# Moving conditioning rows between the first three feed-forwards, and their loads to another queue

## The chip, the cores and the metric

The kernel runs on one core of one Trainium2 chip. The metric is the device time of one execution in microseconds (us). A core has five engines that run side by side: TensorE (PE in the profile) multiplies matrices, VectorE (DVE) and ScalarE (ACT) work elementwise, GpSimd (POOL) does so more slowly, and SyncE (SP) only issues DMA transfers. Each engine takes its own instructions in a fixed order and waits at the first one that isn't ready. Transfers are carried out by 16 DMA engines, whichever engine issued them.

## The reference, cut to what matters

Two layers with their own weights are applied to 128 context tokens and 512 latent tokens of width 1024. Each layer is feed-forward, token mixing, feed-forward, and each of these three has its own shift, scale and gate, which come from the conditioning vector:

```python
def layer(x, cond, p, ...):
    mods = (silu(cond) @ p['w_ada'] + p['b_ada']).reshape(cond.shape[0], 9, 1, D_MODEL)
    sh1, sc1, g1, sh2, sc2, g2, sh3, sc3, g3 = [mods[:, i] for i in range(9)]
    h = modulate(rmsnorm(x, p['norm_ffn1']), sh1, sc1)
    x = x + 0.5 * g1 * swiglu(h, p['w_ffn1_in'], p['w_ffn1_out'])
    h = modulate(rmsnorm(x, p['norm_mix']), sh2, sc2)
    y, kv = token_mix(h, p, ...)
    x = x + g2 * y
    h = modulate(rmsnorm(x, p['norm_ffn2']), sh3, sc3)
    x = x + 0.5 * g3 * swiglu(h, p['w_ffn2_in'], p['w_ffn2_out'])
```

`swiglu` has a hidden width of 2816. The product of the conditioning with `w_ada` gives 9216 values per layer and conditioning vector; there are two vectors, one for context and one for latent tokens.

## The kernel before, in words

**Stages.** The kernel runs, in time, feed-forward 1 (layer 0, about 20 to 531 us in the profile), mixing 1, feed-forward 2 (layer 0, about 821 to 1303 us), feed-forward 3 (layer 1, about 1303 to 1745 us), mixing 2, and feed-forward 4 (layer 1, about 2033 to 2475 us). All 640 tokens lie on the free axis, and the whole activation stays on the chip; the weights stream past in loads of 128x512 floats (`load_raw`, line 159, issued by SP, nine buffers).

**A feed-forward** (`ffn`) treats the 22 column blocks of the hidden width one after the other; one such block is a *pair* here (gate and up part). The pairs are cut into five parts of 5, 5, 4, 4 and 4 (`PARTS`). After each part come eight *outputs* (line 517 and 528), which multiply the part's activations with the output weights and add the result to `x`. So a feed-forward is ten stretches in turn: pairs 1, outputs 1, ..., pairs 5, outputs 5. The residual update of the outputs needs the gate, so the gate must be known before outputs 1. The last outputs also prepare the next norm (`nx.tile`).

Every float32 weight and activation is split in two numbers of fewer bits, `hi` on ACT and `lo` on DVE (lines 174 and 175), and three products are made. DVE also forms sums of weight blocks (line 608), takes results out of the accumulators and applies the gating (lines 622 to 642 and 550).

**Conditioning rows.** The products with `w_ada` that aren't needed at the very start are made on DVE, in *steps* (`ada_steps`, lines 268 and 270). A step loads 128x1024 floats of `w_ada` (512 KB) into one of two buffers (tag `KS`, which the mixing uses too), and multiplies and sums them with each of the two conditioning vectors: two long DVE instructions. Four steps make a chunk of 512 of the 9216 columns; chunks 2j and 2j+1 hold row j of the nine. Steps wait in a list (`Pump`), and `ffn` takes them from it: a pair counts 2 and an output 1, times the feed-forward's rate in `RATES`, and whenever the sum reaches 1 a step is written into the program. A feed-forward counts 22 x 2 + 40 = 84 in all. The loads were issued by SP, in one queue with the weights.

**Order on an engine.** The framework's planner fixes each engine's order when the program is built: whenever an engine comes free by its estimate, it takes the instruction that is ready and stands earliest in the program's text. So a step can run earlier than its place in the text, in a gap that the planner sees on DVE. At run time the order is fixed.

Of the kernel before, what the change touches and what calls it, by code (L numbers as in the profile page):

```python
# [22 lines left out]
POOLD = ()  # L23
SHO = range(8)
SPREAD = 3
RATES = (0.8, 0.8, 0.55)
WLATE = 4
P1A, P0B, P1B = 1, 2, 2
D = 1024
# [53 lines left out]
def hybrid_step(ctx: ExitStack, tc: tile.TileContext, x_in, cc_in, cb_in, w_ada0, w_ada, pv_in, lam_in, w_fin, w_fout, w_min, w_mout,  # L83
                cache_in, ident_in, rope_in, cnt_in, sel_in,
                y_out, ngk, ngv, ndk, ndv):
    nc = tc.nc
    V, S, G, PE = nc.vector, nc.scalar, nc.gpsimd, nc.tensor
# [13 lines left out]
    def nm(s):  # L101
        uid[0] += 1
        return f"{s}_{uid[0]}"
# [4 lines left out]
    def T(dt=F32):  # L108
        return tp.tile([128, UW], dt, tag="t", name=nm("t"))
# [11 lines left out]
    def PS():  # L121
        return psS.tile([128, 2, 512], F32, tag="S", name=nm("S"))

    def PH():
        return psH.tile([128, 512], F32, tag="H", name=nm("H"))

    def PF():
        return psF.tile([128, 512], F32, tag="F", name=nm("F"))

    def C(shape, dt=F32, name="c"):  # L130
        n = nm(name)
        return const.tile(shape, dt, tag=n, name=n)
# [17 lines left out]
    def raw_tile():  # L150
        return wp.tile([128, 512], F32, tag="raw", name=nm("raw"), bufs=RAWB)

    def load_raw(src):

        n, r = src.shape[-1], []
        for c in range(0, n, 512):
            w = min(512, n - c)
            t = raw_tile()
            nc.sync.dma_start(t[:, :w], src[:, c:c + w])
            r.append(t[:, :w])  # L160
        return r

    class Weights:
# [5 lines left out]
        @staticmethod  # L169
        def piece(src, eng=None):  # L170
            n = src.shape[-1]
            hi = wp.tile([128, 512], F32R, tag="hi", name=nm("hi"), bufs=HLB)
            lo = wp.tile([128, 512], F32R, tag="lo", name=nm("lo"), bufs=HLB)
            S.activation(hi[:, :n], src, AF.Copy)  # L174
            (eng or V).tensor_tensor(out=lo[:, :n], in0=src, in1=hi[:, :n], op=ALU.subtract)  # L175
            return hi, lo
# [45 lines left out]
    mods = [[None] * 18 for _ in range(L)]  # L222

    def bada(l, c):
        b = PV_BADA + l * 72 + 4 * c
        return pv[:, b:b + 4].unsqueeze(2).to_broadcast([128, 4, 2])
# [33 lines left out]
    def ada_steps(l, c):  # L260
        m = []

        def step(b):
            if b == 0:
                m.append(C([128, 4, 2], name="mod"))
            t = sp.tile([128, 1536], F32, tag="KS", name=nm("wa"), bufs=2)
            raw, dump = t[:, :D], t[:, D:].bitcast(mybir.dt.bfloat16)
            nc.sync.dma_start(raw, w_ada[l, 4 * c + b])
            for i, o in enumerate((dump, raw)):
                V.scalar_tensor_tensor(out=o, in0=raw, scalar=1.0, in1=rows[i], op0=ALU.mult, op1=ALU.mult,  # L270
                                       accum_out=m[0][:, b, i:i + 1])
            if b == 3:
                V.tensor_tensor(out=m[0], in0=m[0], in1=bada(l, c), op=ALU.add)
                mods[l][c] = m[0]

        return [lambda b=b: step(b) for b in range(4)]
# [10 lines left out]
    def gate_tiles(l, sub):  # L287

        if sub == 1:
            return [mods[l][2 * (3 * sub + 2) + h] for h in range(2)]  # L290
        r = []
        for h in range(2):
            t = C([128, 4, 2], name="gate")
            V.tensor_scalar(out=t, in0=mods[l][2 * (3 * sub + 2) + h], scalar1=-0.5, scalar2=None, op0=ALU.mult)
            r.append(t)
        return r
# [199 lines left out]
    def product(ps, piece, act, start):  # L496

        hi, lo = piece
        for k in range(4):
            w0, w1 = hi[:, k * 128:(k + 1) * 128], lo[:, k * 128:(k + 1) * 128]  # L500
            ah, al = act[k][:, 0], act[k][:, 1]
            for p, (w_, a) in enumerate(((w0, ah), (w0, al), (w1, ah))):
                PE.matmul(ps, w_, a, start=start and k == 0 and p == 0, stop=k == 3 and p == 2, skip_group_check=True)  # L503
# [28 lines left out]
    def ffn(l, sub, norm, nxt, pump, prate):  # L532
# [11 lines left out]
        def activation(i, g, u, cb):  # L544

            lb = HW + HN
            for a, b, c in ((0, NC, cb), (NC, lb, lb)):
                S.activation(g[:, a:b], g[:, a:b], AF.Silu, bias=g[:, c:c + 1])  # L548
            for a, b, c in ((0, NC, cb), (NC, lb, lb)):
                V.scalar_tensor_tensor(out=u[:, a:b], in0=u[:, a:b], scalar=u[:, c:c + 1], in1=g[:, a:b],  # L550
                                       op0=ALU.add, op1=ALU.mult)
            hi, lo = U(), E(F32R)
            split(*[t[:, :N].rearrange("p (h n) -> p h n", h=2) for t in (hi, lo)], FastNorm.view(u)[:, :, :HN])
            acts[i] = (hi, lo)
            tick(2.0)
# [43 lines left out]
        def pair(i, first):  # L599


            a11, a12 = load_raw(wi[i, 0])
            a21, a22 = load_raw(wi[i, 1])
            s3 = raw_tile()
            piece = Weights.piece

            def add(o, a, b):
                V.tensor_tensor(out=o, in0=a, in1=b, op=ALU.add)  # L608

            A, B, D = PF()[:, :HW], PH()[:, :HW], PS()[:, 0, :HW]  # L610
            g, u = T(), T()
            w = piece(a11)
            product(A, w, norm.get("B11"), True)
            S.activation(g[:, :HW], A, AF.Copy)
            w = piece(a12)
            add(s3, a11, a21)
            add(a21, a21, a22)
            add(a11, a21, a11)
            product(B, w, norm.get("B21"), True)
            if first:  # L620
                norm.stats_sum()
            V.tensor_tensor(out=g[:, :HW], in0=B, in1=g[:, :HW], op=ALU.add)
            w = piece(a11)
            product(A, w, norm.get("N2"), False)
            S.activation(u[:, :HW], A, AF.Copy)
            w = piece(s3)
            add(a12, a11, a12)
            product(D, w, norm.get("T3"), True)
            S.activation(u[:, HW:], D, AF.Copy)
            if first:  # L630
                norm.stats_spread()
            w = piece(a21)
            product(A, w, norm.get("N1"), False)
            V.tensor_tensor(out=u[:, HW:], in0=A, in1=u[:, HW:], op=ALU.add)
            w = piece(a22)
            product(D, w, norm.get("T4"), False)
            V.tensor_tensor(out=u[:, :HW], in0=D, in1=u[:, :HW], op=ALU.add)
            w = piece(a12)
            product(A, w, norm.get("B22"), False)
            V.tensor_tensor(out=g[:, HW:], in0=A, in1=norm.R[:, HW:], op=ALU.mult)  # L640
            V.tensor_tensor(out=g[:, :HW], in0=g[:, :HW], in1=norm.R[:, :HW], op=ALU.mult)
            V.tensor_tensor(out=u, in0=u, in1=norm.R, op=ALU.mult)  # L642
            activation(i, g, u, HN)
# [64 lines left out]
        gate = None  # L708
        for k0, k1 in PARTS:
            for i in range(k0, k1):  # L710
                if l == 0 and sub == 0 and i < NPLAIN:
                    plain_pair(i)
                    if i == 0:
                        for k in range(4):
                            norm.late(k)
                else:
                    pair(i, i == 0)
            gate = gate or gate_tiles(l, sub)
            nx = nxt() if k1 == NP else None
            if k1 == NP and nx is None:  # L720
                last_out(k0, k1, gate)
            else:
                for d in ORDER:
                    out(k0, k1, d, gate, nx)
# [677 lines left out]
    nx = FastNorm(0, 0)  # L1402
# [24 lines left out]
    pump = Pump()  # L1427

    def ada_all(l, cs):
        for c in cs:  # L1430
            pump.add(ada_steps(l, c))

    ada_all(0, (4, 5, 8, 9, 6, 7, 10, 11, 14, 15, 12, 13))
    nx = ffn(0, 0, nx, lambda: Norm(0, 1), pump, RATES[0])
    pump.step(1000)
    cache = load_cache(0)
    lambdas()
    nx = mix(0, nx, lambda: FastNorm(0, 2), cache)
    cache = load_cache(1)
    rows = silu_rows()  # L1440
    ada_all(0, (16, 17))
    ada_all(1, (2, 3, 0, 1, 4, 5, 8, 9, 6, 7))
    nx = ffn(0, 2, nx, lambda: (pump.step(8), FastNorm(1, 0))[1], pump, RATES[1])
    pump.step(1000)
    ada_all(1, (10, 11, 14, 15, 12, 13, 16, 17))
    nx = ffn(1, 0, nx, lambda: Norm(1, 1), pump, RATES[2])
    pump.step(1000)
    nx = mix(1, nx, lambda: FastNorm(1, 2), cache)
# [113 lines left out]
```

## Time and profile before

| | |
|---|---|
| median of 3 runs | 2497.93 us (2492.87, 2497.93, 2497.96) |
| profiled execution | 2492.2 us, of which the span from first to last instruction is 2490.4 us |
| mean granted TensorE clock | 0.977 of full |
| busy share of the span: PE, DVE, ACT, POOL | 95%, 85%, 49%, 13% |

The terms of a forecast are read from the profiled execution. The three runs lie up to 5.1 us apart, so the comparison of two kernels goes by medians. An engine's busy share is a mean over stages with different limits.

### The profile page before, as it was taken

To read this page: it belongs to the slowest core of one execution; us is meant where nothing else is said; L and a number is where in the kernel's file an instruction comes from. 1 tells how busy PE (TensorE), PEld (TensorE's weight loads), DVE (VectorE), ACT (ScalarE), POOL (GpSimd) and SP (SyncE) were. 2 spreads that over 40 slices of the span, in tenths; PEclk is the share of its full clock that TensorE was granted. 3 is DMA by queue.
4 is the path that set the end of the run, shared out by engine and by line. 5 is a ranking of instruction groups with operands and counts; after the bars stand their busy time and mean duration, and the time that the engine had idled before them with its cause. 6 is when DMAs were issued, how large, how long until landed. Compare 5 with 4: busy or idle time off the path is not lost. (4 is left out here: it accounts for less than half of the span.)

```text
span 2490.4 us, 42262 instructions
## 1 busy us (share of the span) xinstructions
PE 2360.5 (95%) x15497; PEld 2290.3 (92%) x15497; DVE 2108.2 (85%) x3978; ACT 1213.3 (49%) x2447; POOL 315.2 (13%) x373
## 2 busy tenths in 40 slices
PE   7799999999998999998989999999999989999998
PEld 4798998999988899998979999999998979999997
DVE  5999998867887999999999998778588688767776
ACT  3534333457664634334355344445576565434434
POOL 3100000034233100000030000002422330000002
PEclk8999999999999999999989999999999989999999
DMA  7354443223423144554423453222243112223223
GB/s 267 109 169 139 156 156 117 86 80 122 136 75 123 60 153 125 160 161 147 128 81 104 155 150 96 69 85 85 76 154 105 51 39 80 82 78 97 81 73 98
DMA packets 142671, 280.70 MB, mean 113 GB/s; under 512 B 15360, under 2 KB 33664, under 8 KB 142464
## 3 DMA queue, kind: packets, MB, share of 16 engines
q1 hardware_dynamic: 142464, 278.01, 35.0%
q8 instruction: 122, 2.00, 0.3%
q14 instruction: 85, 0.70, 0.1%
HBM read 263.00 MB, written 14.94 MB: 112 GB/s over the span
## 5 line engine op out<-in xcount | busy, mean ns | idle before, releaser
L174 ACT ACTIVATE hi<-raw 128x512 fp32r<-128x512 f32 (+2 forms) x954 | 569.3, 605 | 874.2 <-PE S L135 359.4
L503 PE MATMUL F<-u,hi 128*128 128x322 f32 x2752 | 634.7, 318 | 33.0 <-ACT hi L174 31.1
L175 DVE TENSOR_TENSOR lo<-raw,hi 128x512 fp32r<-128x512 f32 (+1 forms) x874 | 565.2, 659 | 114.2 <-ACT hi L174 110.4
L135 PE MATMUL S<-u,hi 128*128 128x320 f32 (+3 forms) x2144 | 485.2, 317 | 35.5 <-DVE x L517 12.9
L503 PEld LDWEIGHTS F<-u,hi 128*128 128x128 f32 x2752 | 469.3, 192 | 41.7 <-ACT hi L174 34.3
L503 PE MATMUL F<-u,lo 128*128 128x322 f32 x1376 | 432.9, 315 | 10.5 <-DVE lo L175 10.5
L135 PE MATMUL S<-u,lo 128*128 128x320 f32 (+3 forms) x1776 | 419.3, 312 | 3.2 <-DVE lo L175 2.3
L135 PEld LDWEIGHTS S<-u,hi 128*128 128x128 f32 x2144 | 361.4, 193 | 46.9 <-issue 13.3
L270 DVE SCALAR_TENSOR_TENSOR wa<-wa,sc 128x1024 bf16<-128x1024 f32 (+1 forms) x264 | 323.5, 1233 | 9.7 <-DMA wa<-in_w_ada_dram 6.3
L135 PE MATMUL S<-e,hi 128*128 128x320 f32 (+2 forms) x1408 | 327.8, 310 | 1.1 <-DVE e L197 0.8
L503 PE MATMUL S<-u,hi 128*128 128x322 f32 x1376 | 316.1, 315 | 2.6 <-DVE x L528 2.3
L135 PEld LDWEIGHTS S<-u,lo 128*128 128x128 f32 x1776 | 305.1, 191 | 4.5 <-DVE lo L175 3.3
L503 PEld LDWEIGHTS F<-u,lo 128*128 128x128 f32 x1376 | 267.0, 194 | 13.8 <-DVE lo L175 13.1
L608 DVE TENSOR_TENSOR raw<-raw,raw 128x512 f32<-128x512 f32 x344 | 239.7, 697 | 5.2 <-DMA raw<-in_w_fin_dram 2.1
L135 PE MATMUL F<-u,hi 128*128 128x320 f32 (+1 forms) x1056 | 239.2, 318 | 1.5 <-DVE x L517 0.8
L503 PEld LDWEIGHTS S<-u,hi 128*128 128x128 f32 x1376 | 234.2, 191 | 5.7 <-ACT hi L174 5.0
L135 PEld LDWEIGHTS S<-e,hi 128*128 128x128 f32 x1408 | 236.6, 188 | 2.9 <-DVE e L197 2.5
L503 PE MATMUL S<-u,lo 128*128 128x322 f32 x688 | 215.3, 313 | 1.4 <-DVE lo L175 1.4
L528 DVE SCALAR_TENSOR_TENSOR x<-S,gate,x 128x128 f32<-128x128 f32 (+1 forms) x304 | 152.6, 544 | 53.0 <-PE S L135 52.1
L135 PEld LDWEIGHTS F<-u,hi 128*128 128x128 f32 x1056 | 178.6, 193 | 3.9 <-DVE x L517 0.8
L135 PE MATMUL F<-u,lo 128*128 128x320 f32 (+1 forms) x528 | 157.8, 318 | 0.0
L503 PE MATMUL H<-u,hi 128*128 128x322 f32 x688 | 156.0, 313 | 1.7 <-ACT hi L174 1.7
(229 smaller groups left out, 3032.8 us busy)
## 6 DMA issues: line engine op xcount, KB each, us to landing
raw<-in_w_fin_dram SPq DMA_DIRECT2D x352, 256.0 KB
wa<-in_w_ada_dram SPq DMA_DIRECT2D x132, 512.0 KB
raw<-in_w_fout_dram SPq DMA_DIRECT2D x168, 256.0 KB
raw<-in_w_min_dram SPq DMA_DIRECT2D x72, 256.0 KB
u<-in_w_ada_dram SPq DMA_DIRECT2D x24, 256.0 KB
KS<-kd SPq DMA_DIRECT2D x16, 384.0 KB
raw<-in_w_mout_dram SPq DMA_DIRECT2D x24, 256.0 KB
kd<-t SPq DMA_DIRECT2D x8, 640.0 KB
```

The source lines that it names most:

```text
L135: PE.matmul(out, lhsT, rhs, start=start, stop=stop)
L174: S.activation(hi[:, :n], src, AF.Copy)
L175: (eng or V).tensor_tensor(out=lo[:, :n], in0=src, in1=hi[:, :n], op=ALU.subtract)
L270: V.scalar_tensor_tensor(out=o, in0=raw, scalar=1.0, in1=rows[i], op0=ALU.mult, op1=ALU.mult, accum_out=m[0][:, b, i:i + 1])
L503: PE.matmul(ps, w_, a, start=start and k == 0 and p == 0, stop=k == 3 and p == 2, skip_group_check=True)
L528: V.scalar_tensor_tensor(out=x[d][:, a:b], in0=w[:, a:b], scalar=g[:, d % 4, c:c + 1], in1=x[d][:, a:b], op0=ALU.mult, op1=ALU.add)
L608: V.tensor_tensor(out=o, in0=a, in1=b, op=ALU.add)
```

## The change

The loads of the conditioning steps are issued by POOL (`G`) and no longer by SP. The rate of feed-forward 1 goes from 0.8 to 0.6 steps per count with the same 12 chunks, that of feed-forward 2 from 0.8 to 0.42 and from 12 chunks to 8, that of feed-forward 3 from 0.55 to 0.6 and from 8 chunks to 12. Since at the lower rates the chunks of the gate aren't complete when the gate is built, a loop takes steps from the list until they are. Before the norm that follows feed-forward 2, all that is left in the list is written out, and no longer 8 steps at most.

```diff
-RATES = (0.8, 0.8, 0.55)
+RATES = (0.6, 0.42, 0.6)
...
-            nc.sync.dma_start(raw, w_ada[l, 4 * c + b])
+            G.dma_start(raw, w_ada[l, 4 * c + b])
...
+            while gate is None and mods[l][2 * (3 * sub + 2) + 1] is None:
+                pump.step()
             gate = gate or gate_tiles(l, sub)
...
     ada_all(0, (16, 17))
-    ada_all(1, (2, 3, 0, 1, 4, 5, 8, 9, 6, 7))
-    nx = ffn(0, 2, nx, lambda: (pump.step(8), FastNorm(1, 0))[1], pump, RATES[1])
+    ada_all(1, (2, 3, 0, 1, 4, 5))
+    nx = ffn(0, 2, nx, lambda: (pump.step(1000), FastNorm(1, 0))[1], pump, RATES[1])
     pump.step(1000)
-    ada_all(1, (10, 11, 14, 15, 12, 13, 16, 17))
+    ada_all(1, (8, 9, 6, 7, 10, 11, 14, 15, 12, 13, 16, 17))
     nx = ffn(1, 0, nx, lambda: Norm(1, 1), pump, RATES[2])
```

## Rows read from the trace of the kernel before

**Rows 1.** The page's first part: busy time, share of the span, instructions.

```profile
PE 2360.5 (95%) x15497; PEld 2290.3 (92%) x15497; DVE 2108.2 (85%) x3978; ACT 1213.3 (49%) x2447; POOL 315.2 (13%) x373
```

**Rows 2.** Windows (length; PE, PEld, DVE, ACT, POOL busy; clock, DMA), feed-forwards 1 to 4.

```profile
167.80:444.90 277.10, 260.69 (x1718) 256.11 (x1717) 264.38 (x491) 108.01 (x203) 2.98 (x9) 0.99 0.43 135
926.80:1206.50 279.70, 263.12 (x1719) 258.29 (x1718) 274.14 (x506) 108.29 (x204) 1.84 (x6) 0.98 0.46 145
1403.60:1659.00 255.40, 255.38 (x1717) 254.14 (x1717) 218.50 (x398) 109.29 (x202) 2.10 (x7) 1.00 0.33 102
2139.70:2395.40 255.70, 255.37 (x1718) 253.50 (x1717) 194.01 (x343) 109.87 (x201) 0.00 (x0) 1.00 0.27 81
```

**Rows 3.** The same windows of feed-forwards 2 and 3, conditioning steps alone.

```profile
926.80:1206.50 279.70, 92.51 (x152) 0.98 0.46 145
1403.60:1659.00 255.40, 27.96 (x46) 1.00 0.33 102
```

**Rows 4.** Waits of PE, 920 to 1260 us: total, times, longest.

```profile
PE F L503 <- ACT hi L174: 10.9, 4, 3.5
PE F L503 <- DVE lo L175: 3.9, 3, 1.4
```

**Rows 5.** Windows, feed-forward 3, pairs 2 and outputs 2, columns as rows 2.

```profile
1403.60:1466.10 62.50, 62.50 (x421) 62.48 (x421) 61.83 (x113) 32.97 (x63) 1.92 (x4) 1.00 0.37 113
1466.10:1501.40 35.30, 35.30 (x243) 35.30 (x241) 34.39 (x69) 9.25 (x19) 0.18 (x3) 1.00 0.56 175
```

**Rows 6.** The two windows of rows 5, conditioning steps alone.

```profile
1403.60:1466.10 62.50, 11.03 (x18) 1.00 0.37 113
1466.10:1501.40 35.30, 16.93 (x28) 1.00 0.56 175
```

**Rows 7.** Windows, feed-forward 4 (no steps): pairs 2, pairs 4, outputs 4.

```profile
2139.70:2202.60 62.90, 62.90 (x423) 62.50 (x422) 53.96 (x95) 33.66 (x63) 0.00 (x0) 1.00 0.27 82
...
2316.60:2367.20 50.60, 50.47 (x339) 50.05 (x338) 41.40 (x72) 26.86 (x50) 0.00 (x0) 1.00 0.33 100
2367.20:2395.40 28.20, 28.17 (x193) 27.91 (x193) 18.45 (x33) 6.53 (x10) 0.00 (x0) 1.00 0.15 48
```

**Rows 8.** Windows, conditioning steps alone, mixing 1 to the end of feed-forward 2.

```profile
540.00:1178.00 638.00, 119.68 (x192) 0.98 0.38 124
1178.00:1305.00 127.00, 25.65 (x42) 0.96 0.34 109
```

**Rows 9.** Windows, feed-forward 1 from the third pair on; its outputs 5.

```profile
77.40:531.00 453.60, 424.17 (x2782) 416.80 (x2780) 422.71 (x782) 192.82 (x369) 23.34 (x38) 0.98 0.41 129
...
495.40:531.00 35.60, 35.33 (x237) 34.45 (x235) 29.27 (x47) 22.07 (x41) 17.10 (x25) 1.00 0.24 74
```

**Rows 10.** The conditioning buffers' instructions: ns min/median/max; idle before them (us, times).

```profile
L270 DVE SCALAR_TENSOR_TENSOR wa<-wa,sc x264: 1208/1217/2586, 38.5 to 1500.0; 128x1024 bf16<-128x1024 f32 x123, 128x1024 f32<-128x1024 f32 x9
...
  DMA wa<-in_w_ada_dram: 6.3, 6
```

**Rows 11.** Waits of SP's own queue, whole span: total, times, longest.

```profile
SPq L268 <- DVE wa L270: 453.9, 121, 19.3
```

**Rows 12.** Timeline of SP: issues in the start and in outputs 2 of feed-forward 3.

```profile
43.35 1.48 SPq L268 DMA_DIRECT2D wa<-in_w_ada_dram  x2
...
1491.76 0.33 SPq L268 DMA_DIRECT2D wa<-in_w_ada_dram  x1
```

**Rows 13.** Timeline of DVE: the first use of these two loads.

```profile
46.95 1.23 DVE L270 SCALAR_TENSOR_TENSOR wa<-wa,sc 128x1024 bf16<-128x1024 f32 x1 [2.48 <-DMA wa<-in_w_ada_dram]
...
1496.14 1.23 DVE L270 SCALAR_TENSOR_TENSOR wa<-wa,sc 128x1024 bf16<-128x1024 f32 x1 [0.40 <-DMA wa<-in_w_ada_dram]
```

**Rows 14.** POOL's smallest copies, whole span: ns min/median/max.

```profile
L423 POOL COPY t<-sh x32: 179/392/3382, 56.4 to 2034.4; 128x4 f32<-128x4 f32 x32
```

**Rows 15.** Windows, 5 us of the start, columns as rows 2.

```profile
20.00:25.00 5.00, 1.80 (x7) 1.12 (x7) 4.95 (x6) 5.00 (x13) 4.05 (x3) 0.95 1.04 396
```

**Rows 16.** Timeline of PE, where the first pair's second half begins.

```profile
52.65 0.91 PE L135 MATMUL S<-u,hi 128*128 128x322 f32 x2 [6.11 <-POOL u L416]
```

## Prediction

> **What bounds the kernel now.** The page's busy shares come first [rows 1]: PE is busy 95% of the span, so only what keeps PE waiting can move the end; DVE, at 85% on average, may do so in places. To see where, I cut the same work out of each feed-forward: pairs 2 to outputs 4, six stretches with equal matmuls [rows 2]. PE's count is 1717 to 1719 in all four, yet they take 277.1, 279.7, 255.4 and 255.7 us. The last two run at PE's own pace (PE busy 255.4 of 255.4 and of 255.7). The first two are longer by 21.6 and 24.2 us over a mean of 255.5, and there DVE is busy 264.4 of 277.1 and 274.1 of 279.7 us: in these stretches the end is set by DVE.
>
> What fills DVE is the conditioning steps: 92.5 us in that part of feed-forward 2, 28.0 us in feed-forward 3 [rows 3]. In the view of waits, PE waits for ACT's `hi` (10.9 us in four waits) and for DVE's `lo` (3.9 us in three) in feed-forward 2 [rows 4]; the same view of feed-forwards 3 and 4 lists no wait of PE in their stretch. 14.8 of the 24.2 us are these waits; I read the rest as short gaps and as matmuls after a wait at a lower clock (granted 0.98 against 1.00 [rows 2]).
>
> **Room on DVE.** A step is two instructions of about 1.22 us [rows 10], say 2.44 us. The windows by stretch show how many steps fit before PE has to wait. Pairs 2 of feed-forward 3: 61.83 us of DVE less 11.03 of steps leaves 50.8 of 62.5, room for 11.7 us, 4.8 steps; outputs 2: 34.39 less 16.93 in 35.3, 17.8 us or 7.3 steps [rows 5, 6]. PE was busy throughout in both, with 4.5 and 7 steps in them. From feed-forward 4: pairs of four blocks, 9.2 us or 3.8 steps; outputs after them, 9.75 us or 4.0 [rows 7]. Outputs 5, with the norm: 35.6 less 29.27, 2.6 steps [rows 9]. From outputs 1 to outputs 5 that is 7.3 + 4.8 + 7.3 + 3.8 + 4.0 + 3.8 + 4.0 + 3.8 + 2.6 = 41.4 steps.
>
> **The change part by part.**
>
> *Feed-forward 1, rate 0.8 to 0.6.* Its 48 steps stay. By the tenth count 8 were written before; now 6, and the new loop adds the other 2, since the gate (chunks 4 and 5) needs all 8. The remaining 40 were written by count 60, the end of pairs 4, which is 8 steps in pairs 2 (5 x 2 x 0.8) against room for 4.8; now they are spread to count 77, the start of outputs 5, with 6 in pairs 2. 40 fit into 41.4, so hardly anything is left over on DVE. The sum over the whole feed-forward says the same: 453.6 us with 422.7 of DVE [rows 9]; less 21.6 it would be 432.0, and DVE busy 97.8% of it, between the 98.9% and 97.4% that PE stood without a wait [rows 5]. That is the very edge, and steps that are written into a fixed place don't always meet a gap: I take 16 of 21.6 us, with ends 8 and 24 (above 21.6, since pairs 1 lose two steps, 4.9 us, to outputs 1).
>
> *Feed-forward 2, rate 0.8 to 0.42, 12 chunks to 8.* The 48 steps of before were done by 1178 us (192 instructions, four to a step, from 540 on), and then 42 more instructions, ten to eleven steps of feed-forward 3, ran before feed-forward 2 was over [rows 8]. So the planner draws steps forward into gaps, and what hurt is not how many there are but that those of feed-forward 2 stood ahead of the pairs' own work. With 32 steps at 0.42 that ends: after the gate's 8, 24 steps come to 3.4 in each outputs 1 and 2 and 4.2 in pairs 2, all below the room. Gaps are then filled from feed-forward 3. Of 24.2 us I take 23, ends 15 and 26.
>
> *Feed-forward 3, 8 chunks to 12.* 80 steps in both feed-forwards together stand against 8 for the gate plus twice about 41: they fit, as fill. Its pairs 3 to outputs 4, empty of steps now, get some 15. Filled stretches cost PE nothing in rows 5; I take +1, ends 0 and 6 (two steps too many, 4.9 us).
>
> *Loads from SP to POOL, 132 of them.* SP now stands 453.9 us in all, 121 times, before such a load until DVE frees one of the two buffers [rows 11], and the weight loads behind it stand too. That goes. It is worth little by itself, since feed-forward 3 has the same queue and no wait of PE; I count 0, ends 0 and -5, a part of the 10.9 us of `hi` waits [rows 4]. On POOL a load waiting for its buffer holds up what is behind it: nothing between the start and the last outputs (POOL busy 1.8 to 3.0 us in 277 [rows 2]), but there the squares and shift copies for the next norm (17.1 us of POOL in 35.6 [rows 9]), and in the mixings `lo` pieces. A planner that was right about DVE's times puts such a load where its buffer is free. Included in the next term.
>
> *How late a load lands.* From SP's issue to DVE's use, where DVE stood waiting: 3.6 us at the start and 4.4 us in outputs 2 [rows 12, 13]. DVE's waits for such loads are 6.3 us in the whole run [rows 10], so there is slack. No load is issued by POOL in this trace. The nearest row is POOL's smallest copy: 0.18 us at best, 0.39 in the median, 3.38 at worst [rows 14]; if POOL is held up like this when it issues, a load comes 0.2 to 3.2 us later. It matters in the outputs, where a step follows the other every 5 us: 7 + 7 + 4 + 4 + 2 in three feed-forwards, 72 steps. 0.2 us on each, none hidden, is 15 us. With the slack I take +2, ends 0 and 15. The Trainium skill, "SBUF — State Buffer", section "Who interferes with whom", speaks against this edit: a transfer issued from GpSimd has its descriptors written by GpSimd, which the port it shares with VectorE can starve, and it advises the other queues. It also says that VectorE's two-input operations, which fill DVE here, contend with GpSimd's reads and not its writes. The stretched copies of rows 14 agree with the first for reads; for loads no row here shows it. The same page's section "A bandwidth-pool intuition that's wrong" has a transfer of 0.62 us take 3.1 us beside a VectorE copy; 2.5 us on 72 steps would be an estimated 180 us.
>
> *Start.* In the first 35 us the DMA engines are full, near 400 GB/s [rows 15]. The first two conditioning loads no longer queue behind the activations and can go first: 1.05 MB, 2.6 us later for what PE waits for. The two after them lie in the chain that ends in a 6.11 us wait of PE [rows 16], DVE having waited 2.48 us for one [rows 13]; 3.2 us more at worst. I take +1, ends 0 and 6.
>
> **Sum.** -16 - 23 + 1 + 0 + 2 + 1 = -35 us on the span of 2490.4, so 2455.4, and 1.8 us more for the execution: 2457. The median of the runs is 5.7 us above the profiled execution; by it, 2497.9 - 35 = 2463. I forecast 2461.
>
> **The rivals.**
>
> *Feed-forward 1 gives nothing back.* For it: 40 steps in 41.4 is no room, and a burst of two stands ahead of its outputs 1. Against: nothing else of its cost grows. Without the 16 us: 2497.9 - 19 = 2479. With the ends of the small terms, 2485.
>
> *POOL's loads come late, slower.* Place: the outputs' 72 steps. DVE takes its instructions in order, so each microsecond that it stands for a load delays the residual updates and `lo` pieces behind it, and PE has two accumulators there. 35 / 72 = 0.5 us per step beyond the slack undoes the gain. If one load in four is held like the longest copy, 0.8 us on average, it is 58 us: 2497.9 - 37 + 58 = 2519. For it: the copies of rows 14, and DVE is at its fullest there. Against: 6.3 us of waits in 132 steps. The rule of the Trainium skill's page "SBUF — State Buffer" named above is this rival's mechanism; no row here shows it for a load.
>
> *The rates don't matter.* The planner already runs steps before their place [rows 8]; if it also held them back, the order on DVE would stay: 2498. Against: feed-forwards 1 and 2 differ from 3 by rate alone, and that shows 24 us.
>
> **Chances.** The forecast (2446 to 2470): 0.60. Feed-forward 1 gives little, or small terms take half (2470 to 2490): 0.21. The order stays or gain and loss cancel: 0.07. POOL's loads late: 0.12. Two kernels that differ by under 0.2%, 5 us, can't be told apart by this measurement. Faster by more 0.81, within 0.07, slower 0.12. The range 2446 to 2488 leaves the slower cases and the sliver next to them outside.
>
> **What would show it.** Right: pairs 2 to outputs 4 of feed-forwards 1 and 2 near 261 and 256 us, PE without waits for `hi` in the second, step instructions in pairs 3 to outputs 4 of feed-forward 3, SP's wait for the buffers gone. Wrong: DVE's idle time before steps, until the load's arrival, well over 6.3 us; outputs longer than 35.4; PE's 6.11 us wait in the start grown; POOL's squares late before feed-forwards 2 and 3.

## The result, and the profile after

The changed kernel takes 2461.7 us (median of four runs, 2457.4 to 2463.5) against 2495.4 us for the kernel before (four runs, 2492.0 to 2498.0): a ratio of 0.9863 [0.9842, 0.9884], faster by 1.4%. The forecast was 2461. Its profiled execution took 2460.2 us with a span of 2458.3, so the span is 32.1 us shorter than before, where -35 was summed.

The page's first part. PE's busy time fell by 11 us with the same 15497 matmuls, DVE's is the same as in [rows 1], and POOL has 132 instructions more, the loads:

```profile
PE 2349.6 (96%) x15497; PEld 2284.3 (93%) x15497; DVE 2107.5 (86%) x3978; ACT 1214.4 (49%) x2447; POOL 384.9 (16%) x505
```

The windows of pairs 2 to outputs 4 of the four feed-forwards, columns as in [rows 2]:

```profile
173.20:428.80 255.60, 254.28 (x1718) 253.42 (x1717) 253.31 (x469) 109.17 (x203) 15.52 (x30) 1.00 0.45 141
914.80:1173.80 259.00, 255.75 (x1719) 253.92 (x1718) 253.16 (x470) 108.61 (x202) 20.56 (x35) 1.00 0.43 139
1371.70:1627.70 256.00, 255.18 (x1718) 254.23 (x1717) 236.81 (x435) 109.24 (x202) 13.52 (x28) 1.00 0.39 120
2107.20:2362.70 255.50, 255.36 (x1718) 253.55 (x1717) 194.09 (x343) 110.00 (x201) 0.00 (x0) 1.00 0.26 81
```

277.1, 279.7, 255.4 and 255.7 us became 255.6, 259.0, 256.0 and 255.5: the first two, which DVE set, now run almost at PE's pace. The same windows of feed-forwards 1 to 3 with the steps alone (DVE, then POOL's issues of the loads):

```profile
173.20:428.80 255.60, 70.92 (x116) 15.52 (x30) 1.00 0.45 141
914.80:1173.80 259.00, 69.60 (x114) 15.17 (x29) 1.00 0.43 139
1371.70:1627.70 256.00, 49.97 (x82) 10.04 (x19) 1.00 0.39 120
```

Step work in feed-forward 2 fell from 92.5 to 69.6 us, and in feed-forward 3 it rose from 28.0 to 50.0 [rows 3]; there it costs PE 0.6 us. In the view of PE's waits for feed-forward 2 (909 to 1175 us: total, times, longest), `hi` and `lo` of [rows 4] are gone, and three short entries are left, four waits in all:

```profile
PE F L503 <- DVE t L634: 1.2, 1, 1.2
PE S L135 <- DVE e L197: 1.0, 1, 1.0
PE S L135 <- DVE x L528: 1.0, 2, 0.7
```

Ahead of these stretches the picture differs. First the start of feed-forward 1, on DVE, PE and POOL (start, length, what; in brackets the idle time before it and what ended it):

```profile
41.13 1.23 DVE L270 SCALAR_TENSOR_TENSOR wa<-wa,sc 128x1024 bf16<-128x1024 f32 x1 [1.65 <-ACT sc L256]
50.35 1.23 DVE L270 SCALAR_TENSOR_TENSOR wa<-wa,sc 128x1024 bf16<-128x1024 f32 x1 [3.21 <-DMA wa<-in_w_ada_dram]
56.53 0.91 PE L135 MATMUL S<-u,hi 128*128 128x322 f32 x2 [7.33 <-POOL u L416]
61.84 3.48 POOL L416 CAST u<-shc 128x4 fp32r<-128x4 f32 x8 [1.81 <-DVE shc L197]
63.62 0.56 PE L135 MATMUL S<-u,hi 128*128 128x322 f32 x2 [1.17 <-POOL u L416]
```

The step that began at 46.95 [rows 13] begins at 50.35, PE's wait of 6.11 us [rows 16] is 7.33, and a second one follows. By the third pair the kernel is 5.4 us late: 82.8 against 77.4 us [rows 9]. Then pairs 1, outputs 1 and pairs 5 of feed-forward 1, after the change:

```profile
82.80:129.60 46.80, 39.81 (x254) 39.58 (x253) 45.96 (x88) 26.71 (x56) 3.61 (x7) 0.93 0.25 79
129.60:173.20 43.60, 39.19 (x242) 37.52 (x241) 40.80 (x84) 9.49 (x19) 4.75 (x9) 0.92 0.62 197
428.80:483.20 54.40, 52.02 (x338) 51.41 (x337) 51.70 (x96) 26.22 (x50) 2.84 (x12) 0.97 0.38 121
```

and the same three before it, which the rows ahead of the prediction don't show:

```profile
77.40:132.70 55.30, 42.64 (x254) 41.28 (x253) 53.31 (x104) 26.16 (x55) 3.27 (x4) 0.88 0.35 110
132.70:167.80 35.10, 35.10 (x242) 35.00 (x241) 34.28 (x71) 9.76 (x21) 0.00 (x0) 1.00 0.65 201
444.90:495.40 50.50, 50.42 (x339) 49.97 (x338) 41.47 (x72) 26.82 (x50) 0.00 (x0) 1.00 0.34 100
```

Pairs 1 gained 8.5 us and outputs 1 lost 8.5: together 90.4 before and after. Pairs 5, empty of steps before, now hold four and are 3.9 us longer.

Last, the loads: their issues on POOL (ns min/median/max), the idle time of POOL and of DVE on their account (us, times), the time from issue to landing, and the largest wait of SP's queue, before and after:

```profile
L268 POOL DMA_DIRECT2D wa<-in_w_ada_dram x132: 527/527/755, 1.3 to 1539.3; - x132
...
  DVE wa L270: 945.2, 117
...
  DMA wa<-in_w_ada_dram: 8.8, 9
...
DMA to landing us min/median/max: 3.6/3.9/7.2
```

```profile
SPq L159 <- DVE lo L175: 1064.9, 460, 22.8
...
SPq L159 <- DVE lo L175: 1375.5, 525, 22.8
```

SP's 453.9 us before such loads [rows 11] are gone, but SP stands about as long elsewhere in its queue: its wait for a weight buffer that `lo` frees grew from 1064.9 to 1375.5 us, and that for one that the sums of line 608 free from 97.0 to 203.4 us.

The span's difference adds up from the windows: +5.4 to the third pair, 0 in pairs 1 and outputs 1, -21.5, +3.9 in pairs 5, -20.7 in feed-forward 2, +0.6 in feed-forward 3, and +0.2 in everything between and behind them.

### The profile page after: what moved, and what is told of

It is laid out like the page before. It is cut to its first block, busy times and chain, and to the rows that moved or that the text cites. A ratio compares the mean times of both kernels' runs of the same rounds, so it can differ in the third digit from the quotient of the medians.

```text
span 2458.3 us, 42308 instructions
## 1 busy us (share of the span) xinstructions
PE 2349.6 (96%) x15497; PEld 2284.3 (93%) x15497; DVE 2107.5 (86%) x3978; ACT 1214.4 (49%) x2447; POOL 384.9 (16%) x505
## 5 line engine op out<-in xcount | busy, mean ns | idle before, releaser
L268 POOL DMA_DIRECT2D wa<-in_w_ada_dram x132 | 70.5, 534 | 974.3 <-DVE wa L270 945.2
## 6 DMA issues: line engine op xcount, KB each, us to landing
raw<-in_w_fin_dram SPq DMA_DIRECT2D x352, 256.0 KB
raw<-in_w_fout_dram SPq DMA_DIRECT2D x168, 256.0 KB
raw<-in_w_min_dram SPq DMA_DIRECT2D x72, 256.0 KB
u<-in_w_ada_dram SPq DMA_DIRECT2D x24, 256.0 KB
raw<-in_w_mout_dram SPq DMA_DIRECT2D x24, 256.0 KB
```

The source lines that it names most:

```text
L268: G.dma_start(raw, w_ada[l, 4 * c + b])
```

## The experiments

The theory after the result: the two lower rates alone gain, by letting DVE do the pairs' and outputs' own work first; the new queue gives nothing and costs the 5 us of the start; the move of four chunks isn't needed. The rivals: the queue has a share in the gain (SP's wait is gone, and so are PE's waits for `hi`), or it is the move that relieves feed-forward 2. Experiments 1 to 4 ran beside a median before of 2496.45 us (19 runs), 5 to 8 beside 2494.45 (7), 9 to 12 beside 2498.12 (9).

**1. The changed kernel with its loads on SP.**

```diff
-            G.dma_start(raw, w_ada[l, 4 * c + b])
+            nc.sync.dma_start(raw, w_ada[l, 4 * c + b])
```

> The changed kernel with its new rates and chunk lists, but with the loads of the conditioning steps issued by SP again. Theory (the rates and the move of chunks made the gain, the queue nothing but a later start): pairs 2 to outputs 4 of feed-forwards 1 and 2 stay near 255.6 and 259.0 us, the third pair starts at 77.4 us again and not at 82.8, and the whole is about 5 us faster than the changed kernel, near 2457 us. Rival (freeing the weight loads from the queue behind the conditioning loads made part of it): PE's waits for hi come back, the two stretches are 5 us or more longer, and the whole is 2467 us or above.

2454.75 us, 0.9826 [0.9811, 0.9841], span 2453.8. The windows of feed-forwards 1 and 2, then SP's wait for the steps' buffers (total, times, longest):

```profile
170.50:426.40 255.90, 254.54 (x1718) 253.34 (x1717) 253.68 (x470) 109.63 (x205) 0.00 (x0) 1.00 0.45 141
914.10:1172.60 258.50, 255.60 (x1718) 253.94 (x1717) 252.74 (x469) 109.14 (x202) 3.45 (x6) 1.00 0.45 139
```

```profile
SPq L268 <- DVE wa L270: 325.7, 120, 23.2
```

SP waits for the buffers again, 325.7 us, and both feed-forwards keep their gain; PE's waits for `hi` in feed-forward 2 don't come back. The third pair begins at 78.0 us instead of 82.8. So the queue has no share in the gain.

The late start looks like the queue's price, but it isn't kept: pairs 2 of feed-forward 2 begin at 914.1 us here and at 914.8 in the changed kernel. The two spans differ by 4.5 us, and 2.9 of them lie in one later stretch, from the first matmul of line 503 in feed-forward 4 to its pairs 2: 106.6 us in the changed kernel at a mean granted clock of 0.97, and 103.7 here at 1.00. The changed kernel run again (9) takes 103.8 there, so these 2.9 us aren't the queue's either.

**2. The kernel before with its loads on POOL, nothing else.**

```diff
-            nc.sync.dma_start(raw, w_ada[l, 4 * c + b])
+            G.dma_start(raw, w_ada[l, 4 * c + b])
```

> The kernel before with one edit: the loads of the conditioning steps are issued by POOL. Theory: the order of the steps on VectorE stays forced, pairs 2 to outputs 4 of feed-forwards 1 and 2 stay near 277 and 280 us, the start costs some 3 to 5 us, and the whole is 2495 to 2501 us. Rival (the queue made the gain): PE's waits for hi vanish and the whole falls below 2480 us.

2501.7 us, 1.0019 [1.0009, 1.0028], span 2496.6. The third pair begins at 82.1 us. Feed-forward 2, with SP's wait gone:

```profile
936.60:1216.40 279.80, 262.79 (x1717) 258.28 (x1717) 274.78 (x508) 108.59 (x204) 21.90 (x44) 0.98 0.46 145
```

279.8 against 279.7 us [rows 2]. Seen from the other side it is the same: the queue alone gains nothing, and by the times it makes this kernel about 5 us slower. At the old rates the late start is kept and grows: 4.7 us at the third pair, 9.8 at pairs 2 of feed-forward 2 (936.6 against 926.8 us [rows 2]), and 6.2 at the end of the span.

**3. The changed kernel with its first four loads on SP.**

```diff
-            G.dma_start(raw, w_ada[l, 4 * c + b])
+            (nc.sync if (l, c) == (0, 1) else G).dma_start(raw, w_ada[l, 4 * c + b])
```

> The changed kernel with the first four conditioning loads, those of the first chunk, issued by SP in their old place and all others by POOL. Theory (the first two loads, 1.05 MB, run ahead of what the start waits for): the activations land 2.65 us earlier, the third pair starts at 77 to 79 us and not at 82.8, and the whole is 4 to 5 us faster than the changed kernel, 2456 to 2458 us. Rival (the later start comes from POOL's own queue, where the shift copies stand behind loads): the third pair starts at 80 us or later and the whole gains 3 us or less.

2459.89 us, 0.9854 [0.9839, 0.9868]; the third pair begins at 84.1 us, so the start isn't mended. These are the rival's numbers, but the trace gives another reason than shift copies behind loads. My theory was that the two loads that no longer queue, and run ahead of the activations, make the start late. That part is right: DVE's first step begins at 38.21 instead of 41.13 us. But another part of the start was missing from it. SP, POOL, DVE and PE in order of time:

```profile
45.56 5.32 SPq L159 DMA_DIRECT2D raw<-in_w_fin_dram  x8
50.59 0.76 POOL L268 DMA_DIRECT2D wa<-in_w_ada_dram  x1
57.57 1.23 DVE L270 SCALAR_TENSOR_TENSOR wa<-wa,sc 128x1024 bf16<-128x1024 f32 x1 [5.04 <-DMA wa<-in_w_ada_dram]
60.77 0.91 PE L135 MATMUL S<-u,hi 128*128 128x322 f32 x2 [4.65 <-POOL u L416]
```

The fifth load, the first on POOL, is issued at 50.59 us, when SP has issued eight weight loads (2 MB) from 45.56 on, and DVE can use it only at 57.57, 7.0 us later. DVE takes its instructions in order, and behind that step stands the `shc` product that POOL's casts and PE wait for.

**4. The changed kernel with the old rates.**

```diff
-RATES = (0.6, 0.42, 0.6)
+RATES = (0.8, 0.8, 0.55)
```

> The changed kernel with the rates 0.8, 0.8, 0.55 of before: four chunks still stand in the list of feed-forward 3, and the loads are issued by POOL. Theory (the rate, that is the place at which a step is written among the pairs, decides): feed-forward 1 takes 277 us again in pairs 2 to outputs 4; feed-forward 2 has its 32 steps written by count 40, so pairs 2 are long (about 68 us) and pairs 4 are at PE's pace, in all 265 to 270 us; the whole is 2480 to 2492 us. Rival (the number of steps in a feed-forward decides): feed-forward 2 stays near 259 us, and the whole is 2474 to 2480 us.

2495.58 us, 0.9996 [0.9987, 1.0006]: nothing is left of the gain, and the whole is a little above the 2480 to 2492 us that I expected. Feed-forwards 1 and 2:

```profile
173.70:456.80 283.10, 264.79 (x1718) 259.18 (x1717) 267.73 (x497) 108.26 (x205) 19.88 (x41) 0.98 0.42 133
938.50:1209.60 271.10, 260.05 (x1719) 256.67 (x1718) 265.87 (x495) 109.35 (x205) 19.79 (x40) 0.99 0.46 142
```

With eight chunks instead of twelve feed-forward 2 at rate 0.8 still takes 271.1 us: its steps are taken as early as before, and it runs free only once they are used up (the windows of pairs 2 and pairs 4: 69.6 and 49.9 us). Moving four chunks gives 8.6 of its 20.7 us at the old rate; the rate gives them all, as 7 shows. Feed-forward 1 takes 283.1 us where I expected 277; in 2, with the same rate, list and queue, it took 279.9, and what makes the difference isn't known.

**5 and 6. One rate at a time**, both on the kernel of experiment 1 (loads on SP). In 5 feed-forward 1 has its old rate. In 6 feed-forwards 2 and 3 have their old rates and chunks.

```diff
 # 5
-RATES = (0.6, 0.42, 0.6)
+RATES = (0.8, 0.42, 0.6)
 # 6
-RATES = (0.6, 0.42, 0.6)
+RATES = (0.6, 0.8, 0.55)
...
-    ada_all(1, (2, 3, 0, 1, 4, 5))
+    ada_all(1, (2, 3, 0, 1, 4, 5, 8, 9, 6, 7))
...
-    ada_all(1, (8, 9, 6, 7, 10, 11, 14, 15, 12, 13, 16, 17))
+    ada_all(1, (10, 11, 14, 15, 12, 13, 16, 17))
```

> All loads issued by SP, the new chunk lists and rates, but feed-forward 1 back at 0.8. Theory (steps written ahead of the pairs' work make VectorE late, and each feed-forward pays for itself): pairs 2 to outputs 4 of feed-forward 1 take 276 to 278 us again, its outputs 1 about 35 and not 44 us, its pairs 5 about 50.4; feed-forward 2 stays near 259 us; the whole is 13 to 20 us slower than with the new rate and all loads on SP, 2468 to 2475 us. Rival (feed-forward 1 was full anyway, so its rate only moves the wait about): 2455 to 2462 us.

> All loads issued by SP, feed-forward 1 at 0.6, feed-forwards 2 and 3 with the chunk lists and rates of before (12 chunks at 0.8, 8 at 0.55). Theory: pairs 2 to outputs 4 of feed-forward 2 take 279 to 281 us again, feed-forward 3 has no steps in pairs 3 to outputs 4; the whole is 20 to 22 us slower than with all edits and SP, 2474 to 2478 us. Rival (part of feed-forward 2's gain comes from feed-forward 1 or from the mixing's end): under 15 us slower.

5: 2475.95 us, 0.9929 [0.9912, 0.9946], span 2473.9. 6: 2479.66 us, 0.9938 [0.9921, 0.9955], span 2478.1. The window of feed-forward 1 in 5, and that of feed-forward 2 in 6:

```profile
166.30:444.90 278.60, 262.24 (x1718) 257.74 (x1717) 265.03 (x491) 107.98 (x203) 2.97 (x9) 0.98 0.43 135
```

```profile
914.80:1194.50 279.70, 263.10 (x1718) 258.36 (x1717) 273.90 (x505) 108.27 (x203) 1.83 (x6) 0.98 0.46 145
```

Each feed-forward goes back to its old time by its own edit, and the other keeps its gain (258.9 us in 5, 256.0 in 6). By medians the first is worth 21 us over experiment 1 and the second 25, both above what I expected (13 to 20, and 20 to 22); both sums run a few us above what the windows show (feed-forward 1 reaches the end of pairs 5 at 495.4 us in 5 and at 479.3 in 1, and 5 began it 2.0 us sooner: 18 us; feed-forward 2: 279.7 less 258.5, 21 us), and the rest is spread over stretches that the edits don't touch.

**7 and 11. The rates alone**: loads on SP and the old chunk lists, so that only the rates, the loop for the gate and the write-out before the norm are left of the change. Run twice.

```diff
-            G.dma_start(raw, w_ada[l, 4 * c + b])
+            nc.sync.dma_start(raw, w_ada[l, 4 * c + b])
...
-    ada_all(1, (2, 3, 0, 1, 4, 5))
+    ada_all(1, (2, 3, 0, 1, 4, 5, 8, 9, 6, 7))
...
-    ada_all(1, (8, 9, 6, 7, 10, 11, 14, 15, 12, 13, 16, 17))
+    ada_all(1, (10, 11, 14, 15, 12, 13, 16, 17))
```

> All loads issued by SP and the new rates, but the chunk lists of before: feed-forward 2 keeps 12 chunks, of which some 35 of 48 steps are written among its pairs and outputs and the rest in one block ahead of its last outputs. Theory (the planner runs steps as fill long before their written place, so only steps written too early cost): the move of the four chunks is needless, the whole is within 4 us of all edits with SP, 2451 to 2459 us. Rival (the block of about 13 steps stands on VectorE ahead of the last outputs, 13 x 2.44 us): 10 us or more slower, with long outputs 5.

> The new rates alone: chunk lists of before and all loads on SP, once more and with more rounds. Expected 2450 to 2457 us, the third pair at 76 to 78 us, and faster than the changed kernel by 5 us or more; if the queue and the move were worth something it would be equal or slower.

7: 2452.3 us, 0.9835 [0.9814, 0.9857]. 11: 2457.11 us, 0.9839 [0.9821, 0.9857]. Their spans are 2451.8 and 2451.9, feed-forward 2 takes 258.8 us in 7: the move of the four chunks is not needed. It even costs a little: from pairs 5 of feed-forward 2 to pairs 2 of feed-forward 3 the kernel takes 193.9 us in 7 and 194.0 in 11, and 197.5 in 1. With twelve chunks listed, 0.42 writes steps into the text at the same pace; those left over stand ahead of the last outputs and are fill.

**8. Feed-forward 2 at rate 0**, on the kernel of experiment 1. All of its steps but the gate's are then written out behind its last pairs.

```diff
-RATES = (0.6, 0.42, 0.6)
+RATES = (0.6, 0.0, 0.6)
```

> All loads issued by SP, the new chunk lists, and the rate of feed-forward 2 set to 0: after the 8 steps that the gate needs, the other 24 are all written in one block ahead of its last outputs. Theory (fill): they still run in VectorE's gaps from outputs 1 on, as before their written place, and the whole is within 4 us of all edits with SP, 2451 to 2459 us, feed-forward 2 perhaps 1 to 3 us shorter in pairs 3 to outputs 4. Rival (the written place decides, late as well as early): a block of 24 steps, 59 us of VectorE, ahead of outputs 5, and 20 us or more slower.

2455.82 us, 0.9844 [0.9829, 0.986], and feed-forward 2 takes 259.0 us. Windows of the steps alone, from outputs 1 to outputs 5 and from outputs 5 into the next feed-forward:

```profile
880.50:1250.10 369.60, 101.52 (x166) 1.00 0.45 141
1224.70:1280.60 55.90, 4.92 (x8) 0.88 0.18 55
```

166 step instructions, 41.5 steps, ran before outputs 5 were over, though the text of these stretches holds none of them: 24 are those of feed-forward 2 that are written behind its pairs, the rest are feed-forward 3's. A step that is written late is drawn forward into gaps; one that is written early displaces the stage's own work. Between 0 and 0.42 no difference shows here.

**9 and 10. The changed kernel again, and with twelve of its loads on SP** (the three chunks of the start; the other 120 stay on POOL):

```diff
-            G.dma_start(raw, w_ada[l, 4 * c + b])
+            (nc.sync if l == 0 and c in (1, 4, 5) else G).dma_start(raw, w_ada[l, 4 * c + b])
```

> The changed kernel as it is, beside the other three of this call. Theory (its queue edit costs the late start, about 5 us): near 2460 us, 5 to 9 us slower than the kernel with the new rates alone in this call. Rival (the queue makes no difference that lasts): within 3 us of it.

> The changed kernel with the first twelve conditioning loads (three chunks, up to the gate's) issued by SP and the other 120 by POOL. Theory (the late start has two causes, the first two loads that run ahead of the activations, 2.65 us, and the gate's loads, which issued by POOL share the DMA engines with weight loads that no longer stand behind them, as the 7 us from issue to use of the fifth load showed when only four were on SP): the third pair starts at 76 to 79 us and the whole is near the kernel with the new rates alone, 2451 to 2458 us. Rival (POOL costs time in the later stages too): the start is mended, but the whole stays above 2458 us.

9: 2460.28 us, 0.9858 [0.9839, 0.9878], span 2459.5, third pair at 81.9 us. 10: 2461.36 us, 0.9861 [0.9842, 0.9881], span 2456.9, third pair at 77.9. Over 11, the kernel with the new rates alone, the changed kernel is 3.2 us slower by the medians, where I expected 5 or more, and 7.6 by the spans. The twelve loads do mend the start, by 4.0 us, which experiment 3 with its four did not. But the time doesn't follow, as the rival said: the span is 2.6 us shorter and the median no shorter. For the late start is gone by then, whatever the queue: pairs 2 of feed-forward 2 begin at 915.9 us in 9 and 913.6 in 10, and with all loads on SP at 916.0 in 7 and 915.8 in 11. What the loads on POOL cost, they cost later, and 3.5 us between these kernels and 11 go to the move of the chunks. One place shows a cost of the loads, feed-forward 2, here in the windows of 10 (pairs 2 to outputs 4, then outputs 3 alone):

```profile
913.60:1175.50 261.90, 257.33 (x1718) 255.34 (x1717) 253.44 (x472) 108.50 (x202) 20.69 (x35) 0.99 0.45 137
1063.50:1095.60 32.10, 30.05 (x195) 29.56 (x194) 28.90 (x54) 6.57 (x11) 2.36 (x5) 0.95 0.41 127
```

With loads on POOL and these rates the stretch took 259.0, 260.3 (in 3), 261.6 and 261.9 us, with all loads on SP 258.5 to 259.3 in six executions; outputs 3 alone take 32.1 us here and 30.3 in the first profile of the changed kernel. What in the queue does this was not tried by itself and stays open.

**12. A still lower rate in feed-forward 1**, on the kernel of 7 and 11:

```diff
-RATES = (0.6, 0.42, 0.6)
+RATES = (0.3, 0.42, 0.6)
```

> The new rates alone on SP, with feed-forward 1 at 0.3 and not 0.6: after the gate's 8 some 20 steps are written among the stretches, and the other 20 in one block behind feed-forward 1. Theory (fill, and a feed-forward 1 whose VectorE is full): its pairs 5 lose their 4 us of wait (50.3 and not 54.4), a few steps run in the mixing, and the whole is 0 to 5 us faster than at 0.6, 2447 to 2455 us. Rival (in a full feed-forward steps that aren't forced are left over and stand ahead of the mixing's work and its buffers): 3 us or more slower, with a later start of feed-forward 2 than 825 us.

2450.04 us (2445.9 to 2458.1), 0.9816 [0.9793, 0.9839], span 2444.2, the lowest of the study. Its interval touches those of 11 and of 9, so as a time the step from 11 is not settled. The trace shows where it comes from. Pairs 5 of feed-forward 1 in 11, then in 12:

```profile
425.70:480.10 54.40, 52.02 (x338) 51.41 (x337) 51.71 (x96) 26.30 (x50) 1.47 (x9) 0.97 0.39 121
422.00:471.90 49.90, 49.90 (x338) 49.90 (x338) 49.29 (x90) 26.78 (x50) 1.38 (x3) 1.00 0.44 134
```

The steps alone, in pairs 5 of 11, then in pairs 5 and outputs 5 of 12:

```profile
425.70:480.10 54.40, 9.79 (x16) 0.97 0.39 121
...
422.00:471.90 49.90, 9.81 (x16) 1.00 0.44 134
471.90:507.20 35.30, 3.67 (x6) 1.00 0.28 85
```

Pairs 5 give back 4.5 us, and another 2.9 come from pairs 1 and outputs 1 (90.0 us together, 92.9 in 11). Six step instructions went over into outputs 5, where the changed kernel runs none. But pairs 5 hold four steps in both kernels, so the 4.5 us aren't a matter of how many steps stand there; what in their order makes them was not tried and stays open. Outputs 5 pay some of it (their last update of `x` begins 34.0 us after their start, 32.0 in the changed kernel), but from the end of pairs 5 to the first matmul of line 503 in feed-forward 2 it is 327.2 us in 12 and 328.9 in 11, so the 4.5 us are kept.

## Why the prediction was right, step by step

| term | forecast | measured |
|---|---|---|
| feed-forward 1 | -16 (-8 to -24) | -17.6 |
| feed-forward 2 | -23 (-15 to -26) | -20.7 |
| feed-forward 3 | +1 (0 to +6) | +0.6 |
| SP's queue freed | 0 (0 to -5) | 0 |
| later landing of POOL's loads | +2 (0 to +15) | within the rows above: DVE's wait grew by 2.5, by 1.7 with SP too |
| start | +1 (0 to +6) | +5.4 at the third pair |
| sum on the span | -35 | -32.1 |

The feed-forward terms are from the third pair to the end of pairs 5, and from pairs 2 to outputs 4; +0.2 lies outside all of them.

**What bounded the kernel** was read rightly: the steps of feed-forwards 1 and 2 stood on DVE ahead of the pairs' own work. Old rates alone undo the whole gain (4), new rates alone make it (7, 11), each feed-forward answers to its own rate (5, 6). The rival that the rates don't matter falls with 4.

**Feed-forward 1.** The term was right by way of two things that I had not put into it. The stretch that I costed gave all of its 21.5 us back, where I took 16 for fear of the "very edge". Two other stretches lost time instead. By the room that I counted, 41.4 steps go from outputs 1 to outputs 5, 2.6 of them in outputs 5; the planner drew the steps forward instead, 42.5 of them between outputs 1 and pairs 5, where by the same count 38.8 have room, and none was left for outputs 5. Outputs 1, with nine and a half steps against room for 7.3, lose what pairs 1 gain: PE waits 4.5 us there, 1.7 of them for the gate, and its granted clock is 0.92, where it was 1.00. Pairs 5, with four steps against room for 3.8, are 3.9 us longer. That a surplus of steps makes these 3.9 us is not shown: in experiment 12 pairs 5 hold four steps too and run at PE's pace. The rival that this feed-forward gives nothing back was wrong: experiment 5 makes it worth some 18 to 21 us.

**Feed-forward 2.** -20.7 for -23. Pairs 2 to outputs 4 come to 259.0 us, not 256; loads on SP leave 258.5 to 259.3, so most of the residue isn't POOL's. DVE is busy 253.2 of 259.0 us there, and PE's waits are those for `t`, `e` and `x` shown above. My reason for moving to eight chunks was idle: the rate alone does it (7), and a rate of 0 would have done as well (8).

**Feed-forward 3** takes twelve chunks as fill for 0.6 us in pairs 2 to outputs 4, as its empty gaps said. The term didn't look ahead of them, where the old lists at the new rates are 3.5 us shorter (7, 11).

**The queue.** I had counted 0 for the freed SP, and the experiments agree on both sides (1, 2). SP's wait was a wait of an engine that had time.

**POOL's loads.** The rival "POOL's loads come late" asked for loads that land 0.5 us or more later on 72 steps. They land 3.9 us after issue in the median, 3.6 at best, where SP's took 3.6 and 4.4 at two places from issue to use [rows 12, 13]. DVE waits 8.8 us for them, nine times, and 8.0 us, seven times, with SP as the issuer (1). So the small copies of [rows 14] were no measure for a load. The stretch of feed-forward 2 that got up to 3 us longer with loads on POOL (9, 10) is what the windows show that may be left of this rival. The trap in the Trainium skill, "SBUF — State Buffer", "Who interferes with whom", didn't close here, although VectorE was busy 253.3 of 255.6 us; the Trainium skill ties it to VectorE's two-port modes, and no row here names a mode. Its other statement, that VectorE's two-input operations contend with GpSimd's reads and not with its writes, is in line with this for loads, and the casts shown under the start agree with it for reads.

**The start** is the term that was mis-sized, at the far end of its bounds: +5.4 us at the third pair for +1. I had named both parts, the loads that run ahead of the activations and the chain through PE's wait, and taken them as small. The first is 2.65 us, all of my 2.6: ACT's first squares begin at 19.32 instead of 16.67 us, and DVE's first step at 41.13 instead of 38.47. The other part is that DVE's wait for the third load grew from 2.48 to 3.21 us, and that POOL's eight casts took 3.48 us where the same eight took 1.05. Two of the eight are stretched, each over a step instruction of DVE that reads two inputs:

```profile
62.30 1.22 DVE L270 SCALAR_TENSOR_TENSOR wa<-wa,sc 128x1024 f32<-128x1024 f32 x1
62.37 1.20 POOL L416 CAST u<-shc 128x4 fp32r<-128x4 f32 x1
63.44 1.22 DVE L270 SCALAR_TENSOR_TENSOR wa<-wa,sc 128x1024 bf16<-128x1024 f32 x1
63.50 1.21 POOL L416 CAST u<-shc 128x4 fp32r<-128x4 f32 x1
```

A third, beside a `lo` of DVE, took 0.58 us, and the other five 0.18 each; in the kernel before, DVE stood idle while the eight ran. Experiment 10 shows that the twelve loads of the start are its cause (77.9 us with them on SP, 77.4 before), and 3 that the first four alone are not. As a part of the sum the figure says less than it seems to: with its third pair at 76.9 us kernel 11 takes 403.2 us from there to the end of pairs 5, the changed kernel 400.4, and by pairs 2 of feed-forward 2 the two are level.

That the sum came out only 3 us off is thus a balance: the start was worse by 4.4 and feed-forward 2 by 2.3, feed-forward 1 was better by 1.6 and feed-forward 3 by 0.4, and the 2 set aside for the landing came on top of windows that already hold it.

## What to carry to other kernels

Filler work that a planner may draw forward belongs late in the program's text: written late it fell into the gaps at no cost (a rate of 0 cost nothing), written early it cost some 18 to 25 us per feed-forward. Count the room stretch by stretch, as idle time of the filling engine where the bounding engine never waits, and look at both ends of the region too: here the middle met the count, and the first and the last stretch didn't. A queue does pacing too: before moving loads out of one, ask what they were behind, because on an idle queue they go ahead of what is needed first, or get in behind a burst that they used to precede. And follow such a delay further before you call it the price: here, at the new rates, 5 us at the third pair were gone 830 us later.

## What the runs showed of the hardware that I had not expected

A 512 KB load issued by POOL landed 3.6 to 7.2 us later, 3.9 in the median, in a kernel where DVE was 99% busy for 256 us on end; for SP the traces give no landing, only the 3.6 and 4.4 us from issue to use. An issue is longer on POOL, 0.53 us against 0.33 on SP. POOL then stood 945 us before its loads in 117 waits, and yet no wait of PE for POOL is listed from 909 to 1175 us. A cast of 128x4 elements on POOL took 0.18 us, and 1.2 us where a step instruction of DVE ran beside it. And one and the same kernel, run twice (7 and 11), gave spans within 0.1 us and medians 4.8 us apart, 3.7 of which the kernel before shows beside them too; so a difference of 3 to 5 us between two kernels here is carried by the windows, not by the times alone.
